# A decoder trunk on one core: the mLSTM stage issued in another order

## The chip, the cores and the metric

The kernel runs on one core of a Trainium2 chip. Its time is the device time of one execution in microseconds (us). Three runs of the kernel before gave 1001.4, 1002.04 and 1003.79 us; their median, 1002.04 us, is what the change is measured against. A difference under 0.3% of it, 3.0 us, is about what a measurement of this kernel can't tell from no change.

Engines are named as the profile names them: PE multiplies matrices (PEld loads its stationary operand), ACT evaluates functions and copies with a scale, DVE is the vector engine, POOL the general-purpose one, SP issues the transfers from memory.

## The reference, cut to what matters

Two layers, 256 tokens of width 1024. Each layer is a feed-forward half step, a token mixer beside a cross-attention, and a second feed-forward half step, every one followed by a layer norm. Layer 1, where the change is, has the mLSTM mixer:

```python
u = x @ w_in_mlstm[j]                       # q, k, v, output gate, 8 gates, cross-attention q
qk = silu(causal_dwconv(qk, qk_conv_w))     # 4 taps
gates = gates + b_gates
log_i, log_f = gates[..., :4], log_sigmoid(gates[..., 4:])
# per head: weights exp(log_d - m_t), log_d = bcum_t - bcum_s + log_i_s for s <= t
sc = einsum('bhtd,bhsd->bhts', q, k) * w_intra
num = einsum('bhts,bhse->bhte', sc, v) + ...
h = num / max(abs(den), exp(-m_t))
h = head_norm(h)
tok = sigmoid(o_pre) * h
mix = concat([tok, cross_attention(q, mem @ w_kv_mem)]) @ w_out
x = layer_norm(alpha * x + mix)
```

## The kernel before, in words

All matrices are fp32. A large product is made of operands split into two exact parts, w_h and w_l (line 98: ACT copies raw to w_h with rounding, line 99; DVE subtracts, line 100), and runs on PE as two or three fp32r products (lines 171 to 182). Small products (attention scores, transposes, decay broadcasts, mLSTM scores and numerators) run as plain fp32, without a split; such a matmul is two PE instructions in the trace.

Weights stream through three raw buffers and five pairs of split buffers, in the order of the list `pieces`; `get` makes the pieces one or two ahead of use. In the mLSTM stage one raw buffer holds the four decay matrices (line 571, `decays`), and another the norm gains (`hnb`) until POOL has multiplied the output gates by them (line 564).

The order on each engine is not written out by hand: the code is recorded in the order in which it is called, and a scheduler of the Tile layer then fixes one sequence for each engine. An engine works through its sequence strictly in order, so an instruction that waits holds all behind it. PSUM has two pools of four banks: `ybank` for long sums and scores, `mbank` for the rest. A bank is given out again when its last reader is done; the reader of a product bank is the pair of `comb` (lines 186 and 187), an ACT copy and a DVE addition.

The mLSTM stage (from line 540; its calls stand in lines 719 to 748) does this:

- output gates and the eight gate columns, then `Xattn`'s query projection (tile xq);
- `gate_rows` (574): a chain of small operations over ACT, DVE and POOL, which leaves running sums and maxima in `rows`;
- `values(h, t)` (697): v, for half h of the heads and token tile t, 24 matmuls of 384 columns (tile v);
- `scores(c)` and `values(c)` of the cross-attention (429, 455): eight instructions of scores each (tile sc), a softmax over ACT and DVE, then transposes (pT) and products (xo);
- `columns` (603): four tiny transposes (tile cols), copied out, and an exponential on ACT;
- `decay(h0)` (612): two heads in one bank; a broadcast matmul with four rows of contraction (tile negm), then for each head two DVE additions of the mask (619), two exponentials (620) and a third (622);
- `qk_piece(n)` (627), six of them, three of k and three of q: two banks of eight product pairs (tile qkp), `comb`, the first tap on ACT (637), three taps on DVE (639), and one silu over both banks on ACT (643);
- `mscores(h)` (648), `numer(t)` (661): scores (tile ms) weighted by the decays, numerators (tile num), denominators and head norm on DVE;
- `tokens(t)` (708): gate times normed head, transposed (tile tk), split into the operand `mix`;
- `OutProj`: `head` (493) multiplies the two chunks of `mix` that come from the cross-attention, `rest` (498) the others (tile yo), with the layer norm half by half.

Of the kernel before, what the change touches and what calls it, by code (L numbers as in the profile page):

```python
# [14 lines left out]
P = 128  # L15
# [16 lines left out]
def trunk(ctx: ExitStack, tc: tile.TileContext, d, out):  # L32
# [23 lines left out]

# [1 line left out]
    pieces = []  # L58

    def downs_after(g, xs):  # L60
        """The groups whose down product follows group g's gate and up."""
        if g < max(xs, 1) or g > NG - TAIL:
            return []
        return list(range(g)) if g == xs else [g - 1]
# [37 lines left out]
    def new_act(name):  # L102
        """[128, chunk, part, token]: the two parts side by side."""
        return actp.tile([P, KC, 2, T], F32R, tag="a", name=name)
# [36 lines left out]

# [1 line left out]
    warm = consts.tile([P, 256], F32R, name="warm")  # L143
# [27 lines left out]
    def mm3(o, a, b, start, stop):  # L171
        """o += a^T b with a, b in two exact parts."""
        ah, al = a
        bh, bl = b
        pe.matmul(o, ah, bh, start=start, stop=False)  # L175
        pe.matmul(o, ah, bl, start=False, stop=False)  # L176
        pe.matmul(o, al, bh, start=False, stop=stop)  # L177

    def mmw(bank, w, a, start, stop):
        """bank = [w_h^T a_h + w_l^T a_h | w_h^T a_l], a's parts side by side."""  # L180
        pe.matmul(bank, w[0], a.rearrange("p c t -> p (c t)"), start=start, stop=False)  # L181
        pe.matmul(bank[:, :T], w[1], a[:, 0], start=False, stop=stop)  # L182

    def comb(o, bank):
        """The sum of a bank's two halves."""
        act.activation(o, bank[:, T:], AF.Copy)  # L186
        dve.tensor_add(o, o, bank[:, :T])  # L187

    def tsl(t):
        return slice(t * P, (t + 1) * P)  # L190
# [3 lines left out]

# [1 line left out]
    def load_ln(i):  # L196
# [46 lines left out]
    def norm_both(i, gb, nx, tail):  # L243
        """tail(t): the last products of tile t; its norm follows, t = 1's transposes later."""
        tr = None
        for t in range(2):
            tail(t)
            tr = ln_finish(i, t, gb, nx)
            if t == 0 and nx is not None:
                tr()  # L250
        cur["x"], cur["pending"] = nx, tr
# [4 lines left out]
    def to_parts(a, k0, n, t, bank):  # L256
        """n chunks of 128 columns, transposed in a bank, into an operand's two parts."""
        bv = bank[:, :n * P].rearrange("p (c t) -> p c t", c=n)
# [3 lines left out]

# [1 line left out]
    def ffn(l, j, xs_groups, i, last=False):  # L264
# [113 lines left out]

# [1 line left out]
    kvs = {}  # L380
# [23 lines left out]
    def proj_ws(w, name, use):  # L404
        """Two 128-column chunks of x @ w, transposed; use(chunk, bank) after each."""
        for c in range(2):
# [66 lines left out]

# [1 line left out]
    ORDER = [6, 7, 0, 1, 2, 3, 4, 5]  # L475

    class OutProj:
# [14 lines left out]

        def head(self):
            self.ws[0] = get("wo", self.l, 0)
            for t in range(2):
                self.part(0, t, (0, 1))

        def rest(self, gb):
            for q in range(1, 4):
# [3 lines left out]
            def tail(t):  # L503
                self.part(1, t, (0, 1))
                for h in range(2):
                    for q in range(2, 4):
# [3 lines left out]

# [1 line left out]
    def conv_mixer(mix, between):  # L512
# [22 lines left out]

# [1 line left out]
    lo, hi, al = slice(0, 64), slice(64, 128), slice(0, 128)  # L537
    HP = [((0, al), (1, lo)), ((1, hi), (2, al)), ((3, al), (4, lo)), ((4, hi), (5, al))]

    def mlstm_mixer(mix, i):  # L540
        hnb = rawp.tile([P, 2048], F32, tag="raw", name="hnb")
        nc.sync.dma_start(hnb[:, :DTOK], bass.AP(tensor=d["hng"].tensor, offset=d["hng"].offset,
                                                 ap=[[0, P], [1, DTOK]]))
        # the output gate, natural; the input and forget gates ride along
        w = [get("wop", q) for q in range(4)]
# [19 lines left out]

        # gates as rows [head, t]
        rows = [zp.tile([P, D], F32, tag="z", name=f"rows{q}").rearrange("p (n t) -> p n t", n=4)
# [6 lines left out]
        def gate_rows():  # L574
# [4 lines left out]
            act.activation(rows[0][:NH, 0:2, :], b[:NH].rearrange("p (m t) -> p m t", m=2), AF.Copy)  # L579
            # log_sigmoid(f) = min(f, 0) - log1p(exp(-|f|)); ln(u) is corrected for u's rounding  # L580
            pool.memset(aa, 1.0)
# [10 lines left out]
            pool.tensor_sub(lf, tt, lf)  # L592
            # running sums and maxima
            dve.tensor_tensor_scan(f, aa, lf, 0.0, op0=ALU.mult, op1=ALU.add)
# [15 lines left out]

        # decay weights, transposed: E[s, t] = exp(a_s - M_t) for t >= s
        def decay(h0):
            nb = mbank(f"negm{h0}")
            for h in (h0, h0 + 1):
                o = nb[:, (h - h0) * T:(h - h0) * T + T]
                pe.matmul(o, ident[:NH, h:h + 1].to_broadcast([NH, P]), e, start=True, stop=True)
                Et = E[h]
                for t in range(2):
                    dve.tensor_add(Et[:, 256 * t:256 * t + P], o[:, tsl(t)], mask)
                    act.activation(Et[:, 256 * t:256 * t + P], Et[:, 256 * t:256 * t + P], AF.Exp,  # L620
                                   bias=cols[:, t, h:h + 1])
                act.activation(Et[:, P:256], o[:, P:], AF.Exp, bias=cols[:, 0, h:h + 1])

        # q and k, convolved, silu'd, transposed: [channel, q or k, chunk, t]
        qk = [hp.tile([P, 2, 2, T], F32, tag="h", name=f"qk{n}") for n in range(3)]
# [31 lines left out]

        # h = num / max(|den|, exp(-m)), head norm
        hn = {}
# [30 lines left out]

        # v, natural, with a column of ones after each head
        v1 = [hp.tile([P, NH, DH + 1], F32, tag="h", name=f"v1_{t}") for t in range(2)]
# [29 lines left out]
        xa.scores(0)  # L722
        values(0, 1)
        xa.scores(1)
        columns()
        decay(0)
        decay(2)
        qk_piece(0)
        xa.values(0)
        qk_piece(1)  # L730
        xa.values(1)
        qk_piece(2)
        qk_piece(3)
        qk_piece(4)
        qk_piece(5)
        values(1, 0)
        mscores(0)
        mscores(1)
        values(1, 1)
        mscores(2)  # L740
        mscores(3)
        numer(0)
        numer(1)
        o = OutProj(1, mix, i)
        tokens(0)
        o.head()
        tokens(1)
        o.rest(load_ln(i))

# [1 line left out]
    def late_loads():  # L751
# [21 lines left out]
    o = OutProj(0, mix, 1)  # L773
    o.head()
    o.rest(gb)
# [5 lines left out]

# [1 line left out]
def _layouts(i):  # L783
# [5 lines left out]
    def colmajor(w, width):  # L789
        """[1024, n*width] -> [n, 128, 8*width]: piece, k in chunk, chunk x column."""  # L790
        n = w.shape[1] // width
# [43 lines left out]
```

## Time and profile before

| What | us |
|---|---|
| median of three runs (1001.4 to 1003.79) | 1002.04 |
| profiled execution, span from first to last instruction | 1004.1 |
| PE busy in it | 986.8 (98%) |
| DVE busy | 664.8 (66%) |
| ACT busy | 530.1 (53%) |

The page gives the span of the profiled execution and no other time of it; it is 2.1 us over the median of the runs and 0.3 us over the longest of them. The mLSTM stage, from the output gates to the first products of the next feed-forward, lies between 680 and 810 us of the span. A busy PE is not PE at its peak: the ends of matmuls are modelled, and the clock granted to PE is a row of its own.

### The profile page before, as it was taken

How to read it: one execution, taken by the hardware profiler on the slowest of the kernel's cores; microseconds unless marked ns; L12 is line 12 of the kernel's file. 1: busy time of each engine (PE TensorE's matmuls, PEld its weight loads, DVE VectorE, ACT ScalarE, POOL GpSimd, SP SyncE). 2: the span in 40 equal slices, each digit the busy share in tenths (PEclk: the TensorE clock that was granted, in tenths of full speed). 3: DMA queues.
4: the chain of work that ended last, by engine and by line, in shares of the span. 5: the costliest groups of instructions: out<-in, count | busy, mean ns of one | idle time of the engine just before them, and what ended most of it. 6: DMA issues, size and time to landing. Idle time of an engine off the chain costs nothing.

```text
span 1004.1 us, 12980 instructions
## 1 busy us (share of the span) xinstructions
PE 986.8 (98%) x5116; PEld 834.7 (83%) x5116; DVE 664.8 (66%) x1010; ACT 530.1 (53%) x851; POOL 39.4 (4%) x52
## 2 busy tenths in 40 slices
PE   8999999999999999999999999999999999999996
PEld 7888888888888888888788888889788788888885
DVE  6685657868677656565866656576478887556555
ACT  6565555447445545556355555535676346454540
POOL 0000000100000000000100000002300110000001
PEclk9999999999999999999999999999799999999999
DMA  8884546455535654644464646434145466546421
GB/s 277 311 295 166 210 168 212 171 228 205 187 130 187 241 201 159 218 155 180 173 246 168 215 162 213 154 111 154 78 149 205 185 236 230 199 158 216 161 84 43
DMA packets 29293, 186.90 MB, mean 186 GB/s; under 512 B 3632, under 2 KB 4656, under 8 KB 8368
## 3 DMA queue, kind: packets, MB, share of 16 engines
q1 hardware_dynamic: 29232, 186.07, 51.7%
q8 instruction: 40, 0.66, 0.2%
q14 instruction: 21, 0.17, 0.1%
HBM read 185.01 MB, written 1.05 MB: 185 GB/s over the span
## 4 chain that ended last, share of the span: by engine, by line
PE 89%; DVE 4%; POOL 2%; DMA 2%; issue 2%; ACT 0%; SPq 0%; POOLq 0%; DVEq 0%; ACTq 0%
PE gu L181 28%; PE gu L182 14%; PE y L177 8%; PE y L175 8%; PE y L176 8%; PE qkp L181 3%; PE gx L175 2%; PE gx L177 2%; PE gx L176 2%; DVE wl L100 1%; PE qkp L182 1%; PE cx L181 1%; PE cg L181 1%; PE cb L181 1%; PE yo L177 1%
## 5 line engine op out<-in xcount | busy, mean ns | idle before, releaser
L100 DVE TENSOR_TENSOR wl<-raw,wh 128x1024 fp32r<-128x1024 f32 (+1 forms) x342 | 400.6, 1195 | 147.6 <-ACT wh L99 146.8
L181 PE MATMUL gu<-x,wh 128*128 128x512 f32 x1216 | 431.1, 399 | 1.4 <-DVE s L187 1.1
L99 ACT ACTIVATE wh<-raw 128x1024 fp32r<-128x1024 f32 (+1 forms) x342 | 338.3, 1032 | 113.4 <-PE y L177 45.0
L182 PE MATMUL gu<-x,wl 128*128 128x256 f32 x1216 | 340.8, 281 | 0.4 <-DVE wl L100 0.2
L181 PEld LDWEIGHTS gu<-x,wh 128*128 128x128 f32 x1216 | 228.5, 188 | 57.4 <-DVE s L187 1.4
L182 PEld LDWEIGHTS gu<-x,wl 128*128 128x128 f32 x1216 | 230.0, 189 | 2.6 <-DVE wl L100 1.0
L175 PE MATMUL y<-wh,h 128*128 128x512 f32 x352 | 138.1, 392 | 0.0
L177 PE MATMUL y<-wh,h 128*128 128x512 f32 x352 | 137.7, 391 | 0.0
L176 PE MATMUL y<-wl,h 128*128 128x512 f32 x352 | 137.2, 390 | 0.0
L187 DVE TENSOR_TENSOR s<-s,gu 128x256 f32<-128x256 f32 x152 | 63.2, 417 | 107.6 <-ACT s L186 107.6
L186 ACT ACTIVATE s<-gu 128x256 f32<-128x256 f32 x152 | 57.4, 379 | 111.4 <-PE gu L182 110.7
L177 PEld LDWEIGHTS y<-wh,h 128*128 128x128 f32 x352 | 66.1, 188 | 14.5
L175 PEld LDWEIGHTS y<-wh,h 128*128 128x128 f32 x352 | 66.1, 188 | 14.0
L176 PEld LDWEIGHTS y<-wl,h 128*128 128x128 f32 x352 | 66.1, 188 | 13.0
L301 ACT ACTIVATE h<-s 128x256 fp32r<-128x256 f32 x76 | 31.7, 417 | 68.2 <-DVE s L298 68.0
L297 ACT ACTIVATE s<-s 128x256 f32<-128x256 f32 x76 | 31.6, 416 | 37.0 <-DVE s L187 37.0
L302 DVE TENSOR_TENSOR h<-s,h 128x256 fp32r<-128x256 f32 x76 | 32.0, 421 | 17.9 <-ACT h L301 17.9
L181 PE MATMUL qkp<-x,wh 128*128 128x512 f32 x96 | 38.6, 438 | 0.0
L175 PE MATMUL gx<-wh,x 128*128 128x512 f32 x96 | 38.2, 398 | 0.2 <-DVE x L261 0.2
L177 PE MATMUL gx<-wh,x 128*128 128x512 f32 x96 | 37.5, 391 | 0.0
L176 PE MATMUL gx<-wl,x 128*128 128x512 f32 x96 | 37.4, 390 | 0.0
L260 ACT ACTIVATE x<-xt 128x512 fp32r<-128x512 f32 x20 | 11.4, 596 | 44.2 <-PE xt L239 43.8
(191 smaller groups left out, 996.1 us busy)
## 6 DMA issues: line engine op xcount, KB each, us to landing
raw<-in_wgu SPq DMA_DIRECT2D x83, 1024.0 KB, 4.8
raw<-in_wd SPq DMA_DIRECT2D x43, 1024.0 KB, 4.8
raw<-in_wconv SPq DMA_DIRECT2D x10, 1024.0 KB, 4.8
raw<-in_wout SPq DMA_DIRECT2D x8, 1024.0 KB, 4.8
raw<-in_wm SPq DMA_DIRECT2D x7, 1024.0 KB, 4.7
gb<-in_lngb SPq DMA_DIRECT2D x6, 1024.0 KB, 4.9
raw<-in_wkv SPq DMA_DIRECT2D x4, 1024.0 KB, 4.9
raw<-in_wop SPq DMA_DIRECT2D x4, 776.0 KB, 4.2
```

Of the source, the lines that this page charges most:

```text
L99: act.activation(h, raw, AF.Copy)
L100: dve.tensor_sub(l, raw, h.bitcast(F32))
L175: pe.matmul(o, ah, bh, start=start, stop=False)
L176: pe.matmul(o, ah, bl, start=False, stop=False)
L177: pe.matmul(o, al, bh, start=False, stop=stop)
L181: pe.matmul(bank, w[0], a.rearrange("p c t -> p (c t)"), start=start, stop=False)
L182: pe.matmul(bank[:, :T], w[1], a[:, 0], start=False, stop=stop)
L186: act.activation(o, bank[:, T:], AF.Copy)
L187: dve.tensor_add(o, o, bank[:, :T])
L297: act.activation(t_[:, :256], t_[:, :256], AF.Silu)
L301: act.activation(hh, t_[:, 256:], AF.Copy)
L302: dve.tensor_sub(hT[g][:, 1, fc, :], t_[:, 256:], hh.bitcast(F32))
```

## The change

The order of the calls of the mLSTM stage is another one. `scores(1)` follows the first q/k piece, `columns` and the four decays are spread between the q/k pieces, one head at a time, and so are `values(0)` and `values(1)` of the cross-attention. The four `mscores` and `numer(0)` follow each other, with `values(1, 1)` between `numer(0)` and `numer(1)`. `head` takes a token tile: that of tile 0 stands ahead of `tokens(0)`, that of tile 1 ahead of `rest`, and `tokens(1)` is called within `rest`, after the second quarter of tile 0. Comments are gone, so lines differ by up to two. The number of matmuls is the same.

```diff
-        def head(self):
-            self.ws[0] = get("wo", self.l, 0)
-            for t in range(2):
-                self.part(0, t, (0, 1))
+        def head(self, t):
+            if t == 0:
+                self.ws[0] = get("wo", self.l, 0)
+            self.part(0, t, (0, 1))
 
-        def rest(self, gb):
+        def rest(self, gb, between=None):
...
             def tail(t):
                 self.part(1, t, (0, 1))
+                if t == 0 and between:
+                    between()
...
-        def decay(h0):
-            nb = mbank(f"negm{h0}")
-            for h in (h0, h0 + 1):
-                o = nb[:, (h - h0) * T:(h - h0) * T + T]
-                pe.matmul(o, ident[:NH, h:h + 1].to_broadcast([NH, P]), e, start=True, stop=True)
-                Et = E[h]
-                for t in range(2):
-                    dve.tensor_add(Et[:, 256 * t:256 * t + P], o[:, tsl(t)], mask)
-                    act.activation(Et[:, 256 * t:256 * t + P], Et[:, 256 * t:256 * t + P], AF.Exp,
-                                   bias=cols[:, t, h:h + 1])
-                act.activation(Et[:, P:256], o[:, P:], AF.Exp, bias=cols[:, 0, h:h + 1])
+        def decay(h):
+            o = mbank(f"negm{h}")[:, :T]
+            pe.matmul(o, ident[:NH, h:h + 1].to_broadcast([NH, P]), e, start=True, stop=True)
+            Et = E[h]
+            for t in range(2):
+                dve.tensor_add(Et[:, 256 * t:256 * t + P], o[:, tsl(t)], mask)
+                act.activation(Et[:, 256 * t:256 * t + P], Et[:, 256 * t:256 * t + P], AF.Exp,
+                               bias=cols[:, t, h:h + 1])
+            act.activation(Et[:, P:256], o[:, P:], AF.Exp, bias=cols[:, 0, h:h + 1])
...
         values(0, 1)
+        qk_piece(0)
         xa.scores(1)
+        qk_piece(1)
         columns()
         decay(0)
+        qk_piece(2)
+        decay(1)
+        xa.values(0)
+        qk_piece(3)
         decay(2)
-        qk_piece(0)
-        xa.values(0)
-        qk_piece(1)
         xa.values(1)
-        qk_piece(2)
-        qk_piece(3)
         qk_piece(4)
+        decay(3)
         qk_piece(5)
         values(1, 0)
-        mscores(0)
-        mscores(1)
+        for h in range(NH):
+            mscores(h)
+        numer(0)
         values(1, 1)
-        mscores(2)
-        mscores(3)
-        numer(0)
         numer(1)
         o = OutProj(1, mix, i)
+        o.head(0)
         tokens(0)
-        o.head()
-        tokens(1)
-        o.rest(load_ln(i))
+        o.head(1)
+        o.rest(load_ln(i), lambda: tokens(1))
```

On PE, where the second scores, the columns and the decay broadcasts stood, just ahead of the first q/k piece, before:

```order
L434 MATMUL sc_10_6040<-kT_1760,xqT_5884 128x256
L434 MATMUL sc_11_6041<-kT_1760,xqT_5884 128x256
L606 MATMUL cols<-ident,rows_5865 128x4
L607 MATMUL cols<-ident,rows_5865 128x4
L606 MATMUL cols<-ident,rows_5865 128x4
L607 MATMUL cols<-ident,rows_5865 128x4
L616 MATMUL negm_6073<-rows_5864,ident 128x256
L616 MATMUL negm_6086<-rows_5864,ident 128x256
L181 MATMUL qkp_0_6109<-x_5562,wh_5955 128x512
```

And with the change, on PE, from the last product of the third q/k piece (wl_6127) to the first products of the fourth (wh_6197), where the second head's broadcast negm_6251 and the transposes of the first attention half now stand:

```order
L182 MATMUL qkp_1_6227<-x_5562,wl_6127 128x256
L616 MATMUL negm_6251<-rows_5864,ident 128x256
L463 MATMUL pT_00_6259<-ident,p_00_5996 128x128 x4
L463 MATMUL pT_01_6267<-ident,p_01_6006 128x128 x4
L181 MATMUL qkp_0_6287<-x_5562,wh_6197 128x512
L468 MATMUL xo_0_6258<-p_00_5996,vm_1761 64x256 x2
L182 MATMUL qkp_0_6287<-x_5562,wl_6198 128x256
```

The scores, columns and broadcasts that stood in one block are now apart, each behind a q/k piece; the scheduler gives pT_00 the bank of the first head's broadcast, and pT_01 the bank of the second head's, negm_6251, so that each waits until DVE and ACT have read that broadcast.

On ACT, the exponentials of the decays (lines 620 and 622) before, with the first copy of a q/k piece (line 186) and its first tap (637) among them:

```order
L609 ACTIVATE ecol<-cols 128x8
L620 ACTIVATE decays<-decays,cols 128x128 x2
L622 ACTIVATE decays<-negm_6073,cols 128x128
L620 ACTIVATE decays<-decays,cols 128x128 x2
L622 ACTIVATE decays<-negm_6086,cols 128x128
L186 ACTIVATE qu_6100<-qkp_0_6109 128x256
L620 ACTIVATE decays<-decays,cols 128x128 x2
L622 ACTIVATE decays<-negm_6073,cols 128x128
L637 ACTIVATE qr_6099<-qu_6100,qcw 128x256
L620 ACTIVATE decays<-decays,cols 128x128 x2
L622 ACTIVATE decays<-negm_6086,cols 128x128
```

With the change, on ACT, from the end of the second q/k piece to the last exponential of the second head (L643 is the silu of a piece, wh_6197 the split of the fourth piece's weights):

```order
L611 ACT_TABLE_LOAD
L611 ACTIVATE ecol<-cols 128x8
L620 ACTIVATE decays<-decays,cols 128x128 x2
L643 ACT_TABLE_LOAD
L643 ACTIVATE qk_5870<-qr_6123 128x512
L622 ACT_TABLE_LOAD
L622 ACTIVATE decays<-negm_6187,cols 128x128
L99 ACTIVATE wh_6197<-raw_6196 128x1024 x2
L186 ACTIVATE qu_6195<-qkp_0_6204 128x256
L186 ACTIVATE qu_6195<-qkp_1_6227 128x256
L620 ACTIVATE decays<-decays,cols 128x128 x2
L622 ACTIVATE decays<-negm_6251,cols 128x128
```

The exponentials, which stood together ahead of the first silu, now alternate with the silus, and the function tables are loaded at each turn: in the mLSTM stage ACT's sequence holds 12 table loads after the output gates where it held 4.

On PE, around the first transposes of the gated heads (tk), before:

```order
L176 MATMUL yo_11_6687<-wl_6489,mix_5705 128x512
L715 MATMUL tk_6648<-ident,og 128x128 x3
L177 MATMUL yo_11_6687<-wh_6488,mix_5705 128x512
L175 MATMUL yo_00_6669<-wh_6662,mix_5705 128x512
L715 MATMUL tk_6655<-ident,og 128x128 x3
L176 MATMUL yo_00_6669<-wl_6663,mix_5705 128x512
```

With the change, at the same place on PE:

```order
L175 MATMUL yo_01_6661<-wh_6490,mix_5705 128x512
L176 MATMUL yo_01_6661<-wl_6491,mix_5705 128x512
L177 MATMUL yo_01_6661<-wh_6490,mix_5705 128x512
L715 MATMUL tk_6672<-ident,og 128x128 x3
L715 MATMUL tk_6679<-ident,og 128x128 x3
L175 MATMUL yo_10_6685<-wh_6490,mix_5705 128x512
```

Before, 23 products of the out-projection stood ahead of the first tk, all of them `head`; now 12 do, those of tile 0, and 40 stand between the transposes of tile 0 and those of tile 1, where 26 stood.

## Rows read from the trace of the kernel before

**Rows 1.** The page: busy time by engine, and the granted clock over 40 slices of the span (in tenths of full speed).

```profile
PE 986.8 (98%) x5116; PEld 834.7 (83%) x5116; DVE 664.8 (66%) x1010; ACT 530.1 (53%) x851; POOL 39.4 (4%) x52
...
PEclk9999999999999999999999999999799999999999
```

**Rows 2.** The view by windows, PE alone: stretch, its length, PE busy (instructions), granted clock, share of the transfer engines, GB/s.

```profile
713.82:717.34 3.52, 2.74 (x16) 1.00 0.00 0
717.34:730.99 13.65, 13.65 (x38) 0.50 0.00 0
730.99:767.58 36.59, 36.59 (x220) 1.00 0.49 163
775.31:782.67 7.36, 7.36 (x41) 1.00 0.48 156
```

**Rows 3.** The timeline of PE: start, duration, line, tiles, count, and the idle time ahead with what ended it.

```profile
713.82 0.70 PE L434 MATMUL sc<-kT,xqT 64*128 64x256 f32 x2
714.97 1.13 PE L434 MATMUL sc<-kT,xqT 64*128 64x256 f32 x6 [0.45 <-ACT p L446]
716.58 0.22 PE L607 MATMUL cols<-ident,rows 4*128 4x4 f32 x1 [0.34 <-POOL rows L598]
716.79 1.52 PE L616 MATMUL negm<-rows,ident 4*128 4x256 f32 x4
719.69 0.63 PE L181 MATMUL qkp<-x,wh 128*128 128x512 f32 x1
720.33 0.63 PE L181 MATMUL qkp<-x,wh 128*128 128x512 f32 x1
...
723.02 1.22 PE L616 MATMUL negm<-rows,ident 4*128 4x256 f32 x2
...
725.11 1.22 PE L616 MATMUL negm<-rows,ident 4*128 4x256 f32 x2
...
735.94 0.40 PE L181 MATMUL qkp<-x,wh 128*128 128x512 f32 x1
736.30 0.40 PE L181 MATMUL qkp<-x,wh 128*128 128x512 f32 x1
```

**Rows 4.** Groups of ACT's instructions in the stretch 713.82 to 767.58: line, operation, tiles, shapes, count, then busy time, mean ns of one, idle time ahead and its releaser.

```profile
L99 ACT ACTIVATE wh<-raw 128x1024 fp32r<-128x1024 f32 (+1 forms) x16 | 15.6, 1001 | 0.6 <-DMA raw<-in_wm 0.6
L637 ACT ACTIVATE qr<-qu,qcw 128x256 f32<-128x256 f32 x12 | 6.1, 505 | 0.7 <-DVE qu L187 0.6
L186 ACT ACTIVATE qu<-qkp 128x256 f32<-128x256 f32 x12 | 4.6, 380 | 10.1 <-PE qkp L182 10.1
L643 ACT ACTIVATE qk<-qr 128x512 f32<-128x512 f32 x5 | 3.1, 628 | 0.1
L620 ACT ACTIVATE decays<-decays,cols 128x128 f32<-128x128 f32 x8 | 2.8, 398 | 0.0
L465 ACT ACTIVATE p<-pT 128x512 f32<-128x512 f32 x4 | 2.2, 591 | 0.1
L622 ACT ACTIVATE decays<-negm,cols 128x128 f32<-128x128 f32 x4 | 1.4, 360 | 0.0
L643 ACT ACT_TABLE_LOAD x1 | 1.3, 1283 | 1.1 <-DVE qr L639 1.1
```

**Rows 5.** The timeline of ACT in the gate chain: a table load and the activation behind it.

```profile
704.92 1.28 ACT L583 ACT_TABLE_LOAD   x1
706.22 0.42 ACT L583 ACTIVATE rows<-rows 4x256 f32<-4x256 f32 x1
```

**Rows 6.** The timeline of DVE: the operations of the softmax, of a q/k piece and of the gate chain.

```profile
714.11 0.68 DVE L596 TENSOR_TENSOR_SCAN rows<-rows 4x256 f32<-4x256 f32 x1 [0.25 <-POOL rows L595]
...
715.48 1.20 DVE L451 TENSOR_SCALAR p<-p,ri 128x256 f32<-128x256 f32 x2
...
717.32 1.28 DVE L441 TENSOR_REDUCE nm<-sc 128x2 f32<-128x512 f32 x2
...
725.63 0.42 DVE L187 TENSOR_TENSOR qu<-qu,qkp 128x256 f32<-128x256 f32 x1 [0.86 <-ACT qu L186]
...
726.86 1.52 DVE L639 SCALAR_TENSOR_TENSOR qr<-qu,qcw,qr 128x253 f32<-128x253 f32 x3
```

**Rows 7.** The timeline of PE where the mLSTM scores, the values between them and the numerators stand.

```profile
767.58 3.73 PE L654 MATMUL ms<-qk 128*128 128x256 f32 x16
771.07 0.42 PE L175 MATMUL v<-wh,x 128*128 128x384 f32 x1
...
775.31 3.73 PE L654 MATMUL ms<-qk 128*128 128x256 f32 x16
778.88 4.09 PE L673 MATMUL num<-v,decays 128*128 128x193 f32 x24
782.67 0.53 PE L175 MATMUL yo<-wh,mix 128*128 128x512 f32 x1
```

**Rows 8.** The timeline of PE around the transposes of the gated heads, and the first product of the feed-forward behind.

```profile
789.13 0.52 PE L715 MATMUL tk<-ident,og 128*128 128x128 f32 x3 [0.89 <-DVE og L712]
...
790.23 0.50 PE L175 MATMUL yo<-wh,mix 128*128 128x512 f32 x1 [0.35 <-DVE og L712]
...
797.72 0.99 PE L715 MATMUL tk<-ident,og 128*128 128x128 f32 x6 [0.73 <-DVE og L712]
...
809.71 0.40 PE L175 MATMUL gx<-wh,x 128*128 128x512 f32 x1
```

More of the change, by code (lines that the diff above doesn't have):

```diff
@@ L773, in trunk @@
     o = OutProj(0, mix, 1)
-    o.head()
+    o.head(0)
+    o.head(1)
     o.rest(gb)
```

## The prediction

> **What bounds the kernel now.** I read the page first: PE is busy for 98% of the span, and the row of its granted clock shows one slice of 40 at seven tenths [rows 1]. So nothing but PE sets the end, and a change of order can win only where PE stood, or ran at the lower of its two levels, 1.2 in place of 2.4 GHz. The windows find that stretch: from 717.34 to 730.99 the granted clock was 0.50, 13.65 us long, with PE busy throughout [rows 2]. The timeline shows what came just before: the second scores, an idle 0.45 us for ACT, the tiny column transposes, 0.34 us for POOL, and the broadcasts with four rows of contraction; PE was busy for 2.74 of 3.52 us [rows 2, 3]. The third view is the end of the stage, where PE waits for the gated heads on DVE, 0.89, 0.35 and 0.73 us [rows 8].
>
> **What the new order takes away.** A product pair took 0.64 us at the low level (719.69 to 720.33) and 0.36 at the high one (735.94 to 736.30) [rows 3]. Of the 38 instructions in the slow stretch 31 are qkp, 15.5 pairs or 5.5 us at the high level. The other 7 are broadcasts: 0.36 us apart at the stretch's start (1.45 us for four, to 718.24, partly slow already); the mLSTM scores, 128 and 256 columns mixed, stood 0.22 apart (3.49 us for 16) [rows 3, 7]. I take 0.30, so 2.1 us. The stretch cost 13.65 - 7.6 = 6.1 us. With both idle times, 6.9 us are to be had.
>
> **What it adds.** Exponentials and silus alternate, so that ACT loads tables 12 times in place of 4; behind the second v product it is 9 in place of 1. One load took 1.283 us [rows 4], so 10.3 us more of ACT in all. ACT has the room in sum: it waited for PE in this stretch for 10.1 us [rows 4]. But it works in order, and PE's banks hang on it, so I walked the new sequences of PE, ACT and DVE side by side with the durations of rows 3, 4 and 6 (times as if on the old span; PE reaches the end of the second v product at 713.8 as before).
>
> PE: first piece to 719.5, scores to 720.7, second piece to 726.4, columns and broadcast to 727.6, third piece to 733.3, second broadcast to 734.1. The third piece needs a bank that DVE frees at 727.0: no wait, by 0.6 us.
>
> DVE (durations from [rows 6]): the splits of the second and third piece's weights now stand ahead of the gate chain, which starts its first exponential at 709.1 in place of 706.2 [rows 5], and the first softmax sums come at 714.4. From there DVE does four multiplications of 0.6, two scans of 0.65, two additions of 0.4, six taps of 0.4, two reductions of 0.6 and three waits for ACT or POOL (0.65, 0.5, 0.5), with smaller ones, and ends the first piece's taps at 724.1.
>
> ACT from 724.1: table 1.28, silu 0.63, copy 0.35, wait for DVE's second softmax until 727.0, tap 0.5, copy 0.35, wait until 728.35, tap 0.5, table 1.28, exponentials behind their masks until 731.0, table 1.28, silu 0.6, table 1.28, the first head's last exponential at 734.65. Then two splits of 1.0, two copies of 0.36, two exponentials of 0.3, and the second head's last one at 738.3.
>
> PE again: pT_00 waits for the 734.65, 0.6 us; pT_01 for the 738.3, 3.15 us; the second pair of xo waits for its copy, which stands behind a split and two taps on ACT (741.25), 0.65 us; the fifth piece waits 0.5 us for a bank of the fourth. Together 4.9 us. The values (4.24 us [rows 7]) then end at 765.3, where before they ended at 767.58.
>
> The clock comes in again here. From 733.4 to 738.9 PE has a four-row broadcast, transposes and 3.75 us of idle time, more than ahead of the fall at 717.34 [rows 2]. I therefore take a second fall. Its price lies between nothing and a repeat of the whole 6.1 us. I take the piece that follows, 5.64 us of products at half speed for about three fifths of it: 3.3 us, less 0.8 of the waits named, which a slower PE no longer feels: 2.5. The values then end at 767.8, 0.2 later than before.
>
> There is a cap on the best case. The last silu, which the third mLSTM scores need, comes at 768.2 in my walk of ACT. Before, without the values between, they would have started at 775.31 - 4.24 = 771.1 [rows 7]. While ACT's chain stays so, the stage can't win more than 2.9 us.
>
> Scores, values and numerators took 15.09 us (767.58 to 782.67 [rows 7]). Four scores in a row and half the numerators are 7.15 + 1.4 us of plain fp32; scores and numerators in a row, 7.36 us, held the granted clock at 1.00 [rows 2]. Same parts, so nothing.
>
> The end of the stage wins: numer(0) starts 4.24 us before numer(1), so DVE has the first gated head some 2.8 us behind the last numerator, about when the 12 products of tile 0 (2.75 us: 26 of them and three transposes filled 790.23 to 796.99 [rows 8], and I take 0.23 each) are done; I leave 0.3 us. The second tile has 40 products, 9.1 us, ahead of its transposes in place of 26; I find DVE done at 794.1 on the old clock, just before them. Of 1.97 us [rows 8] 0.3 stays; another 0.3 goes where fewer products cover the transposes of the normed tile ahead of 809.71. That is -1.4 us. Bounds: nothing, and the whole 1.97.
>
> The first layer's PE sequence is unchanged, and the weights' transfers keep their order; two are issued earlier, which costs nothing while the engines' share in the slow stretch was 0.00 [rows 2].
>
> Sum: +0.2 - 1.4 = -1.2 us. On the profiled span that is 1002.9 of 1004.1; the span stands 2.1 us over the median, so on the median it is 1002.04 - 1.2 = 1000.8.
>
> **A rule that speaks against it.** In this trace the activation behind a load starts 1.30 us after the load starts (704.92 to 706.22) [rows 5], so a switch costs its row. The Trainium skill, page "ScalarE: Activation LUTs", section "What ACT_TABLE_LOAD costs", adds a drain of about 1.38 us to each load of 1.283. The trace agrees with the load and shows no drain. By the page, eight more switches would be an estimated 21 us of ACT in place of 10.3.
>
> **The rivals.**
>
> *The clock holds* (0.22). PE stays at 1.00 through the wait for pT_01. For it: at 788 to 797 idle times of 0.35 to 0.89 left the clock alone. Against: these waits are longer. Then the values end at 765.3: -2.3 - 1.4 = -3.7, 998.3.
>
> *ACT hides its tables* (0.10). If ACT reaches the second head's last exponential by 735, because what I put in series overlaps, PE sees neither wait nor fall, and all comes: -6.9 - 1.4 = -8.3, 993.7. For it: ACT's 10.1 us of waiting in the old order. Against: the chain from 724.1 to 738.3 holds 1.5 us of waits, the rest is work.
>
> *The fall lasts* (0.17). Before, the clock stayed low while single broadcasts cut the products (723.02 and 725.11 [rows 3]), and came back only behind an uncut row of them. In the new order the fourth piece is cut by two pairs of xo, and a broadcast and transposes follow. If the low level reaches past the end of the fourth piece (746), the whole 6.1 is paid again, 3.6 more than I took: +2.4, 1004.4, slower than before.
>
> *A switch costs more than its row* (0.04). The one load ahead of a silu came behind 1.05 us of idle time on ACT, named as a wait for DVE [rows 4]. If ACT must stand for that long at each switch, nine make 9.5 us, the last silu comes at 777.7, 6.6 behind the 771.1, and the end is +6.6 - 1.4 = +5.2, 1007.2. The page named above is this rival's source; the 1.30 us of rows 5 is why it gets so little.
>
> **How the numbers follow.** The forecast, stalls on ACT and a short fall, has 0.47, with 998.5 to 1003 as its own range. A difference of 3.0 us (0.3%) is what the measurement can tell. Faster by more: two thirds of the first rival, the second, and a twentieth of the forecast, 0.15 + 0.10 + 0.05 = 0.30. Slower by more: under half of the third and the fourth, with 0.01 for the forecast, 0.08 + 0.04 + 0.01 = 0.13. The rest, 0.57, is no change that can be told. The range for 8 in 10 leaves out the second rival, the fourth and the outer part of the third: 996.0 to 1005.0.
>
> **What would show it.** Right: nine table loads on ACT between the second v product and the last silu; PE idle before pT_01 by about 3 us with ACT's line 622 as releaser; a granted clock of 0.50 right behind it, shorter than 13.65 us, and none near the first q/k piece; under 0.7 us of idle time left before the tk. Wrong: no wait at pT_01 (then the walk of ACT is wrong), or a clock of 1.00 through it (then the first rival), or a low stretch as long as before.

## The result, and the profile after

The changed kernel took 1005.62 us (median of seven runs, 1004.57 to 1007.44), the kernel before 1001.40 beside it (seven runs, 999.48 to 1003.79): a ratio of 1.0041, with a 95% interval of 1.0027 to 1.0056. It is slower by some 4.2 us; forecast were 1000.8 us in a range of 996.0 to 1005.0, and slower by over 0.3% had a chance of 0.13.

The profiled execution of the changed kernel took 1004.82 us, 1.9 of them outside its span of 1002.9. Of the seven it has the highest mean granted clock, 0.996; the others show 0.993 to 0.995, so the usual execution of the changed kernel runs longer at half clock than the trace read here. Its page, the lines that answer to [rows 1]:

```profile
PE 983.2 (98%) x5116; PEld 830.4 (83%) x5116; DVE 667.3 (67%) x1010; ACT 540.8 (54%) x859; POOL 38.2 (4%) x52
...
PEclk9999999999999999999999999999999999999999
```

ACT has 8 instructions more, the table loads, and 10.7 us more to do. The slice at seven tenths is gone, and the kernel is slower all the same. The windows of PE (length, PE busy, granted clock, share of the transfer engines, GB/s) show a shorter fall in another place than in [rows 2]:

```profile
720.00:731.15 11.15, 10.40 (x60) 1.00 0.00 1
731.15:735.90 4.75, 1.35 (x7) 1.00 0.00 0
735.90:739.30 3.40, 3.06 (x9) 0.50 0.55 188
739.30:766.13 26.83, 26.55 (x145) 1.00 0.36 128
```

From 731.15 on PE is busy for 1.35 of 4.75 us, and behind that runs at half clock for 3.40 us. The timeline of PE says what it stands for (start, duration, line, tiles, count, and the idle time ahead with what ended it); it answers to [rows 3]:

```profile
701.11 0.60 PE L580 MATMUL grows<-ident,gn 128*4 128x128 f32 x4
...
723.88 0.67 PE L616 MATMUL negm<-rows,ident 4*128 4x256 f32 x2
...
725.30 0.50 PE L181 MATMUL qkp<-x,wh 128*128 128x512 f32 x1 [0.75 <-DVE qu L187]
...
731.15 0.69 PE L616 MATMUL negm<-rows,ident 4*128 4x256 f32 x2
...
732.97 0.66 PE L463 MATMUL pT<-ident,p 128*128 128x128 f32 x4 [1.12 <-ACT decays L622]
...
736.24 1.12 PE L463 MATMUL pT<-ident,p 128*128 128x128 f32 x4 [2.62 <-ACT decays L622]
...
737.72 1.83 PE L468 MATMUL xo<-p,vm 128*64 128x256 f32 x4
...
740.84 1.08 PE L468 MATMUL xo<-p,vm 128*64 128x256 f32 x4
```

Both transposes of the first attention half (pT) wait for the decays' last exponentials on line 622. The timeline of ACT shows why these are late (table loads have no tiles); the pair of [rows 5] now stands here at every turn:

```profile
722.60 1.28 ACT L643 ACT_TABLE_LOAD   x1
723.89 0.63 ACT L643 ACTIVATE qk<-qr 128x512 f32<-128x512 f32 x1
...
729.31 1.28 ACT L643 ACT_TABLE_LOAD   x1
730.60 0.63 ACT L643 ACTIVATE qk<-qr 128x512 f32<-128x512 f32 x1
731.25 1.28 ACT L622 ACT_TABLE_LOAD   x1
732.55 0.37 ACT L622 ACTIVATE decays<-negm,cols 128x128 f32<-128x128 f32 x1
732.82 1.99 ACT L99 ACTIVATE wh<-raw 128x1024 fp32r<-128x1024 f32 x2
...
735.82 0.37 ACT L622 ACTIVATE decays<-negm,cols 128x128 f32<-128x128 f32 x1
```

At 729.31 ACT changes to the silus' table for one silu of 0.63 us and at 731.25 back to that of the exponentials; a split of weights (L99) follows. The groups of ACT between 711 and 766 us, the counterpart of [rows 4], have nine loads where one stood:

```profile
L643 ACT ACT_TABLE_LOAD x5 | 6.4, 1283 | 0.1
...
L620 ACT ACT_TABLE_LOAD x2 | 2.6, 1283 | 0.0
...
L611 ACT ACT_TABLE_LOAD x1 | 1.3, 1283 | 0.0
L622 ACT ACT_TABLE_LOAD x1 | 1.3, 1283 | 0.0
```

At the end of the stage PE still waits for the gated heads, 0.73 and 1.19 us, 1.92 in all, against 1.97 in [rows 8]:

```profile
785.02 1.12 PE L715 MATMUL tk<-ident,og 128*128 128x128 f32 x6 [0.73 <-DVE dn L676]
...
796.44 0.99 PE L715 MATMUL tk<-ident,og 128*128 128x128 f32 x6 [1.19 <-DVE og L712]
```

The timeline of DVE has the reason for the 1.19: a split of weights (L100) stands between the norm of the second tile's heads (L687) and their gate (L712). Ahead of the first tile's gate no split stands there; DVE waited 1.26 us for POOL's root, as it did for the second tile.

```profile
782.89 1.25 DVE L687 TENSOR_SCALAR ht<-ht,hmv,hn0r 128x192 f32<-128x192 f32 x4 [1.26 <-POOL hn0r L206]
...
793.44 1.25 DVE L687 TENSOR_SCALAR ht<-ht,hmv,hn1r 128x192 f32<-128x192 f32 x4 [1.26 <-POOL hn1r L206]
794.60 1.22 DVE L100 TENSOR_TENSOR wl<-raw,wh 128x1024 fp32r<-128x1024 f32 x1
795.74 1.02 DVE L712 TENSOR_TENSOR og<-og,ht 128x384 f32<-128x384 f32 x2
```

### The profile page after: what moved, and what is told of

Its sections match the earlier page's. It is cut to its first block, busy times and chain, and to the rows that moved or that the text cites. A ratio compares the mean times of both kernels' runs of the same rounds, so it can differ in the third digit from the quotient of the medians.

```text
span 1002.9 us, 12987 instructions
## 1 busy us (share of the span) xinstructions
PE 983.2 (98%) x5116; PEld 830.4 (83%) x5116; DVE 667.3 (67%) x1010; ACT 540.8 (54%) x859; POOL 38.2 (4%) x52
## 3 DMA queue, kind: packets, MB, share of 16 engines
HBM read 185.01 MB, written 1.05 MB: 186 GB/s over the span
## 4 chain that ended last, share of the span: by engine, by line
PE 88%; DVE 4%; ACT 3%; DMA 2%; POOL 2%; issue 1%; POOLq 0%; DVEq 0%; ACTq 0%
PE gu L181 28%; PE gu L182 14%; PE y L177 8%; PE y L175 8%; PE y L176 8%; PE gx L177 2%; PE gx L176 2%; PE gx L175 2%; PE qkp L181 1%; PE cx L181 1%; PE cb L181 1%; PE cg L181 1%; DMA raw<-in_wm 1%; PE xt L239 1%; PE kb L181 1%
## 5 line engine op out<-in xcount | busy, mean ns | idle before, releaser
L100 DVE TENSOR_TENSOR wl<-raw,wh 128x1024 fp32r<-128x1024 f32 (+1 forms) x342 | 400.6, 1195 | 149.5 <-ACT wh L99 148.8
L99 ACT ACTIVATE wh<-raw 128x1024 fp32r<-128x1024 f32 (+1 forms) x342 | 338.3, 1032 | 112.9 <-PE y L177 48.4
L181 PE MATMUL qkp<-x,wh 128*128 128x512 f32 x96 | 35.0, 405 | 1.0 <-DVE qu L187 1.0
```

Of the source, the lines that this page charges most:

```text
L99: act.activation(h, raw, AF.Copy)
L100: dve.tensor_sub(l, raw, h.bitcast(F32))
```

## The experiments

All are read between three points of PE's timeline: the transposes of the gates (grows), the first of the mLSTM scores (ms), and the first product of the feed-forward behind the stage (gx). "Waits" is the idle time of PE that the timeline names between the first and the last point; "clock" is half the length of the stretches at the granted clock of 0.50. Times in us of each run's profiled execution.

| kernel | grows to ms | ms to gx | sum | waits | clock | ratio to before, 95% |
|---|---|---|---|---|---|---|
| before, the prediction's trace | 63.90 | 42.13 | 106.03 | 2.8 | 6.8 | |
| e1, before again | 59.81 | 42.13 | 101.94 | 3.2 | 1.7 | 0.9993 [0.9982, 1.0004] |
| after | 65.02 | 42.49 | 107.51 | 6.9 | 1.7 | 1.0041 [1.0027, 1.0056] |
| e2, old end | 65.45 | 43.70 | 109.15 | 6.4 | 3.4 | 1.0066 [1.0052, 1.0079] |
| e3, one table | 59.11 | 42.47 | 101.58 | 3.2 | 0 | 0.9982 [0.9971, 0.9994] |
| e4, silus last | 58.56 | 41.64 | 100.20 | 2.5 | 0 | 0.9984 [0.9973, 0.9995] |
| e5, only the end | 59.83 | 41.83 | 101.66 | 2.8 | 1.7 | 0.9991 [0.9979, 1.0003] |
| e6, pT elsewhere | | | 105.91 | 5.2 | 0 | 1.0048 [1.0029, 1.0066] |
| e7, e4 and the gate | 57.77 | 40.87 | 98.64 | 1.0 | 0 | 0.9952 [0.9936, 0.9968] |
| e8, e4 with the old end | 58.28 | 43.80 | 102.08 | 4.4 | 0 | 0.9998 [0.9985, 1.0011] |

(In e6 the first scores stand among the values, so its sum isn't parted.) By the 0.3% that a measurement can tell, e1, e3, e4, e5 and e8 can't be told from the kernel before; the changed kernel, e2 and e6 are slower, e7 is faster. Against the changed kernel's ratio e3 and e4 are 0.6% faster.

### e1: the kernel before, once more

No edit.

> The kernel before, unchanged, run again. The prediction took all it could win from one profiled execution: a stretch of 13.65 us at half clock (6.1 us lost) and, behind 10 us, a start that looks late beside the changed kernel's (first gate rows at 703.68 against 701.11 us). Theory A, that execution was no typical one: this profile starts its gate rows at about 701, its own time lies within 1.5 us of 1001.4, and its slow stretch is shorter than 13 us or absent; the mean clock of the timed runs is above 0.991 in most. Rival B, it was typical: gate rows at 703.7 again, a slow stretch of 13 to 14 us, mean clock 0.991 in nearly all runs, and the own time near 1006.

The profiled execution took 999.6 us, and its gates came at 701.40. PE's windows around the second scores and broadcasts, and the rows of its timeline that answer to [rows 3] and [rows 7]:

```profile
714.86:720.60 5.74, 5.34 (x25) 1.00 0.00 0
720.60:724.20 3.60, 3.60 (x13) 0.53 0.00 0
724.20:761.21 37.01, 37.01 (x222) 1.00 0.48 161
```

```profile
712.69 1.13 PE L434 MATMUL sc<-kT,xqT 64*128 64x256 f32 x6 [0.45 <-ACT p L446]
...
718.68 0.69 PE L616 MATMUL negm<-rows,ident 4*128 4x256 f32 x2 [0.40 <-ACT decays L622]
...
726.59 1.19 PE L468 MATMUL xo<-p,vm 128*64 128x256 f32 x8
...
761.21 2.90 PE L654 MATMUL ms<-qk 128*128 128x256 f32 x12
```

The same program, the same order, the same 0.45 us of waiting: but the clock falls within the 3.60 us of the second window, whose mean of 0.53 makes 3.4 us at 0.50, and not for 13.65 us [rows 2]; that costs 1.7 us. The results list the mean granted clock of every timed execution too. Of 63 of the kernel before, taken with e1 to e4 and with e5 to e8, 43 had 0.995 or more and a median of 999.97 us; 20 had 0.994 or less and a median of 1002.8; three had 0.991, the value of the prediction's trace, and took 1003.88 to 1005.41. The 0.996 of the trace above is the commonest value, in 35 of the 63. So theory A holds, but for the own time, which is 1.8 us from 1001.4 where it had 1.5 at most: if 0.991 stands for the long fall, that is one execution in about twenty. The first trace's span of 1004.1 stands for about 1006 us, if what lies around the span is 1.8 to 2.2 us as in every one of these. That is above each of the three runs it was set beside.

### e2: the changed kernel with the old end

```diff
-        for h in range(NH):
-            mscores(h)
-        numer(0)
-        values(1, 1)
-        numer(1)
+        mscores(0)
+        mscores(1)
+        values(1, 1)
+        mscores(2)
+        mscores(3)
+        numer(0)
+        numer(1)
         o = OutProj(1, mix, i)
-        o.head(0)
         tokens(0)
+        o.head(0)
         o.head(1)
-        o.rest(load_ln(i), lambda: tokens(1))
+        tokens(1)
+        o.rest(load_ln(i))
```

> The changed kernel with the end of the stage as before (scores in pairs around the last values, both numerators together, the gated heads ahead of head). Theory A (the loss is in front, on ACT's queue): the end is worth nothing either way, idle time ahead of the tk 1.9 us as in both traces; time within 1 us of the changed kernel's 1005.6. Rival C (the new end is what costs): 1002.5 or less. The prediction's own term (the new end wins 1.4 us): 1007.

1006.9 us, ratio 1.0066. Rival C is out: the new end is not what costs. Theory A's time, within 1 us of 1005.6, is missed by 0.3. From ms to gx the old end took 43.70 us here and the new one 42.49, 1.2 us for the new end, near the prediction's 1.4. But the ratios' intervals, 1.0052 to 1.0079 and 1.0027 to 1.0056, overlap a little, so that the times alone don't part this from nothing. Two things come on top. The front had a second stretch at half clock, between 726.0 and 729.4, behind a wait of 1.02 us ahead of the third piece where the changed kernel had 0.75 and no fall, as the windows of PE show:

```profile
726.00:729.40 3.40, 3.40 (x12) 0.50 0.02 5
```

And the old end took 1.6 us more here than in the kernel before (42.13, in both of its traces).

### e3: one table for exponentials and silus

```diff
-            act.activation(qk[i][:, which].rearrange("p c t -> p (c t)"), r, AF.Silu)
+            act.activation(qk[i][:, which].rearrange("p c t -> p (c t)"), r, AF.Exp)
```

> The changed kernel with an exponential where the six silus of q and k stand (this changes what is computed: q and k are exp of the convolution in place of silu), so that exponentials and 'silus' share one table. Order of PE as in the changed kernel. Theory A: no table loads between the second v product and the last of the six; pT_00 and pT_01 wait under 0.8 us together (3.74 in the changed kernel), no half clock around 736 us, so about 3.0 + 1.7 us less: 1000.5 to 1001.5. Rival D (the tables are not what holds ACT): waits over 2.5 us stay, 1004 or more.

999.03 us, ratio 0.9982. With PE's order as in the changed kernel, but for a few places (the eight products xo of an attention half now stand together), and no table load between the second v product and the last of the six, both waits ahead of pT are gone, and so is the fall. The windows of PE, and the transposes and products of the first attention half in its timeline:

```profile
730.00:740.00 10.00, 8.91 (x51) 1.00 0.35 115
```

```profile
731.21 1.09 PE L463 MATMUL pT<-ident,p 128*128 128x128 f32 x8
...
733.38 1.57 PE L468 MATMUL xo<-p,vm 128*64 128x256 f32 x8 [1.08 <-ACT p L465]
```

From grows to ms it takes 59.11 us, 5.9 less than the changed kernel. Rival D is out: this shows that the turns between the tables are the cause, and that without them the new order of PE is no slower than the old one. It is not free: without the wait of 1.08 us, the attention's transposes and products take 5.1 us in this trace from start to start and 3.7 in e1; that there is no fall (1.7 us in e1), and 0.7 us less for the scores, makes up for it. The time came out 1.5 us below what I expected: the kernel before took 1000.18 us beside it, 1.2 less than beside the changed kernel, and the eight products of xo take 1.57 us here, where four of them took 1.83 in the changed kernel.

### e4: the true silus, behind the decays

```diff
-            r = tmp(f"qr{n}")
+            r = qk[i][:, which].rearrange("p c t -> p (c t)")
...
-            act.activation(qk[i][:, which].rearrange("p c t -> p (c t)"), r, AF.Silu)
+        zb = sp.tile([P, 1], F32, tag="zb", name="zb", bufs=1)
+
+        def silu(n):
+            if n == 0:
+                dve.tensor_scalar(zb, E[3][:, P:P + 1], 0.0, None, op0=ALU.mult)
+            r = qk[n % 3][:, 1 if n < 3 else 0].rearrange("p c t -> p (c t)")
+            act.activation(r, r, AF.Silu, bias=zb)
...
         decay(0)
+        decay(1)
         qk_piece(2)
-        decay(1)
+        decay(2)
         xa.values(0)
         qk_piece(3)
-        decay(2)
+        decay(3)
         xa.values(1)
+        for n in range(4):
+            silu(n)
         qk_piece(4)
-        decay(3)
+        silu(4)
         qk_piece(5)
+        silu(5)
```

The zero bias hangs on the last head's decay, so that the scheduler, which takes what is ready, can't put a silu among the exponentials.

> The changed kernel with the true silus, but held behind the last decay (a zero column made from the last head's decay is their bias; the convolution is written into the q/k tile itself and the silu done in place) and with the decays one q/k piece earlier (0 and 1 behind the second piece, 2 behind the third, 3 behind the fourth): one table load for silu in place of nine loads. Theory A: PE waits under 1.5 us in all between the second v product and the scores, no half clock; 999.5 to 1001.5. Rival E (small fp32 matmuls at four places let the clock fall whatever ACT does): a half-clock stretch of 3 us or more appears, 1003 or more.

998.79 us, ratio 0.9984: 0.7 us below the range of theory A, and 0.16% below the kernel before, less than a measurement can tell. All that PE waits for, in its timeline:

```profile
726.56 0.50 PE L181 MATMUL qkp<-x,wh 128*128 128x512 f32 x1 [0.82 <-DVE cols L610]
...
734.28 1.56 PE L468 MATMUL xo<-p,vm 128*64 128x256 f32 x8 [0.25 <-ACT p L465]
...
779.46 0.55 PE L722 MATMUL tk<-ident,og 128*128 128x128 f32 x3 [0.50 <-DVE og L719]
...
789.83 0.99 PE L722 MATMUL tk<-ident,og 128*128 128x128 f32 x6 [0.96 <-DVE og L719]
```

No half clock in this trace, though small fp32 matmuls stand at four places: rival E is out for it. What theory A says of the waits (1.07 us between the second v product and the scores) and of the clock holds, with the computation unchanged.

### e5: the kernel before with the new end

The end of e2's diff the other way round, and `head` and `rest` as in the change.

> The kernel before with only the end of the stage changed (four scores and numer(0) ahead of the last values, head per token tile, the second tile's heads within rest). The first queue of the stage is as before, so ACT has one table load there. The prediction gave the new end -1.4 us, bounds 0 and -1.97: ratio 0.9986. Theory F (the new end is worth nothing, since DVE puts splits of weights ahead of the gated heads): ratio 0.9993 to 1.0007, 1.5 to 2.2 us of idle time ahead of the tk. Rival C (the new end costs): above 1.001.

Ratio 0.9991, 0.9979 to 1.0003: the interval holds the prediction's 0.9986 and theory F's nothing, and leaves out rival C. From ms to gx 0.3 us less than before (41.83 against 42.13), with 1.65 us ahead of the tk in place of 1.97. Inconclusive between the two.

### e6: the transposed attention weights in other banks

```diff
-                tb = mbank("pT" + n)
+                tb = ybank("pT" + n)
```

> The changed kernel with the transposed attention weights (pT) in banks of the other PSUM pool, so that they wait for no decay's last exponential; the table loads stay, 8 or 9 of them. Theory G (the loads cost PE only through the bank that pT shares with a broadcast): the 3.74 us ahead of pT go, no half clock near 736, 1000 to 1001.5. Rival H (ACT's queue is the bound, and whatever comes behind it on ACT makes PE wait: the copies of pT, of the q/k pieces, the last silus): PE waits 3 us or more elsewhere, 1003.5 or more.

1006.26 us, ratio 1.0048: as slow as the changed kernel. The timeline of PE, and what ACT does then:

```profile
732.51 0.66 PE L463 MATMUL pT<-ident,p 128*128 128x128 f32 x4
...
734.65 0.49 PE L181 MATMUL qkp<-x,wh 128*128 128x512 f32 x1 [1.48 <-ACT wh L99]
...
735.91 0.39 PE L182 MATMUL qkp<-x,wl 128*128 128x256 f32 x1 [0.76 <-DVE wl L100]
```

```profile
732.00 1.28 ACT L622 ACT_TABLE_LOAD   x1
733.29 0.37 ACT L622 ACTIVATE decays<-negm,cols 128x128 f32<-128x128 f32 x1
733.56 1.99 ACT L99 ACTIVATE wh<-raw 128x1024 fp32r<-128x1024 f32 x2
```

pT no longer waits for line 622, but PE goes on to the next piece, whose weights ACT splits behind the same table loads, and waits there for 2.24 of the 3.74 us. In the trace, which has no half clock, 1.6 us are won between grows and gx (105.91 against 107.51); the runs show nothing of it. Theory G falls by its time; rival H is the nearer one, with 2.9 us of waits ahead of the last score and 5.2 in all. The bank was where the wait showed, and ACT's queue what most of it was for.

### e7: e4, the columns in another bank, and the gate ahead of the root

```diff
-            cb = mbank("cols")
+            cb = ybank("cols")
...
-                dve.tensor_scalar(ht[:, s], ht[:, s], mv[:, h, 0:1], rs[:, h:h + 1],
-                                  op0=ALU.subtract, op1=ALU.mult)
-            hn[t] = ht
+                dve.scalar_tensor_tensor(ht[:, s], ht[:, s], mv[:, h, 0:1], ogs[t][:, s],
+                                         op0=ALU.subtract, op1=ALU.mult)
+            hn[t] = ht, rs
...
-                dve.tensor_mul(og[:, s], og[:, s], hn[t][:, s])
+                ht, rs = hn[t]
+                dve.tensor_tensor(og[:, s].rearrange("p (a e) -> p a e", a=2),
+                                  ht[:, s].rearrange("p (a e) -> p a e", a=2),
+                                  rs[:, 2 * h:2 * h + 2, None].to_broadcast([P, 2, DH]), op=ALU.mult)
```

> The version with the silus behind the decays, and two more edits: the column transposes stand in a bank of the other pool, so that the third piece no longer waits for their copy (0.82 us), and the gate multiplies the centred heads while POOL still computes the square roots, so that behind POOL's wait only one multiplication by the root is left (about 1.1 us in place of 2.27). Theory F (the end hangs on DVE behind POOL): idle time ahead of the tk from 1.46 to under 0.6 us, 1.0 to 1.8 us below the version without the two edits, so about 997.3. Rival I (DVE is busy with splits of weights anyway, and only their order changes): within 0.5 us of 998.8.

996.56 us, ratio 0.9952 with 0.9936 to 0.9968: faster than both kernels, by 4.5 us against the runs of before beside it (1001.09). PE's waits for the gated heads in its timeline, and DVE ahead of the second:

```profile
777.57 0.94 PE L725 MATMUL tk<-ident,og 128*128 128x128 f32 x6
...
787.06 0.99 PE L725 MATMUL tk<-ident,og 128*128 128x128 f32 x6 [0.79 <-DVE og L720]
```

```profile
786.35 1.03 DVE L720 TENSOR_TENSOR og<-ht,hn1r 128x384 f32<-128x384 f32 x2 [0.94 <-POOL hn1r L206]
```

Of the 1.46 us 0.79 are left, not under 0.6, and the 0.82 ahead of the third piece are gone; between grows and gx it is 1.56 us shorter than e4. By the times it is 2.2 us below e4, more than the 1.0 to 1.8 expected; five of e4's executions show a mean clock of 0.996 and none of e7's is under 0.997, so part of that may be the clock. Theory F is the nearer one.

### e8: e4 with the old end

The end as in e2's diff.

> The version with the silus behind the decays, and the end of the stage as before. It prices the end where the front makes PE wait for nothing. Theory F (the end is worth nothing): within 0.7 us of 998.8. The prediction's term: 1000.2, 1.4 us above. Rival C (the new end costs): 998 or less.

1001.22 us, ratio 0.9998 against e4's 0.9984: 1.4 us for the new end, as the prediction's term has it, though the intervals overlap. The timeline of PE has longer waits of the kind of [rows 8]:

```profile
782.22 0.52 PE L722 MATMUL tk<-ident,og 128*128 128x128 f32 x3 [1.12 <-DVE og L719]
...
783.80 0.52 PE L722 MATMUL tk<-ident,og 128*128 128x128 f32 x3 [1.06 <-DVE og L719]
...
788.93 0.50 PE L177 MATMUL yo<-wh,mix 128*128 128x512 f32 x1 [0.72 <-DVE mix L261]
```

Rival C is out here too. The old end takes 43.80 us behind this front and 43.70 behind that of e2, but 42.13 behind the old one. Most of it is PE waiting longer for DVE: the named waits behind the first score are 3.4 us here and 2.8 in e2, against 2.0 before. What makes DVE late there is open; no run here takes it apart.

## Why the prediction was wrong

**The step that failed** is the first term of the sum: "The stretch cost 13.65 - 7.6 = 6.1 us. With both idle times, 6.9 us are to be had." It is right for the execution it was read from, and not for the kernel. The other trace of before loses 1.7 us to its fall, and e1's list of executions, with its mean clock of 0.996 in 35 of 63, says that this is the usual one. So 4.4 us of the 6.1 were not there to be won. From grows to ms the kernel before needs 59.81 us and not 63.90; against the prediction's 64.1 for the changed kernel (63.90 + 0.2) that alone is +4.3 where it had +0.2. With the -1.4 for the end left as it was, the sum is +2.9 us: 1004.3 on the 1001.40 of the runs beside the changed kernel, close to the 1005.62 measured.

The last step hid this: "the span stands 2.1 us over the median, so on the median it is 1002.04 - 1.2". A span and a time were set against each other as if they were the same quantity. With what lies around the span the profiled execution was some 4 us over its median, which should have been explained, not subtracted. Against e1 it is 4.1 us longer between grows and gx, in the very term I was about to spend, and its gates came 2.3 us later; 1.9 of these had gathered in the first 24 us of the span, where PE's named waits are 1.6 us in this trace and 0.45 in e1's, far from the change.

**What held.** The walk of ACT's queue: nine table loads; the last exponential of the first head at 732.92 and that of the second at 736.19 on the new clock, 732.1 and 735.7 by the prediction (its 734.65 and 738.3, less the 2.57 us by which the gates came earlier). Waits of 1.12 and 2.62 us at pT, 3.74 together, where it had 0.6 and 3.15, 3.75 together. A second fall shorter than the first, 3.40 us long, so 1.7 lost in this trace where 2.5 was taken as a net cost; the median of the seven mean clocks, 0.995, stands for some 1 us more. Scores, values and numerators: 15.11 us from the first score to the first product of the out-projection (766.13 to 781.24), 15.09 before [rows 7].

**What else was off.** The third piece was to wait for nothing, with 0.6 us to spare; it waited 0.75 for a bank whose copy on ACT came behind a table load and a silu (722.60 to 724.5), since the softmax kept ACT until 722.6, 1.1 us later than in my walk. The fifth piece waited 0.28, where I had 0.5, and the second pair of xo waited for nothing, where I had 0.65. So it is partly luck that the waits of the front add up to 4.77 us, near the 4.9 of the prediction. Together the changed kernel's front is 65.02 us, 0.9 above the prediction.

**The end** was to win 1.4 us and came out 0.36 longer than before (42.49 against 42.13). Where only the end differs, the traces give the new end 1.2 us (e2 and after), 2.2 (e8 and e4) and 0.3 (before and e5): a gain each time, but of no one size. What I left out is that it does not add to the front's: behind the new front the old end would have been 1.6 us longer. In the trace the idle time did not fall from 1.97 to 0.3 but stayed at 1.92. Of that 1.19 comes from the split of weights that DVE's order has in front of the second tile's gate. The first tile's 0.73 has no split behind it: the first gated head was done at 784.87, 3.6 us behind the last numerator (the out-projection starts at 781.24) and not 2.8, and in that time DVE stood 1.26 us for POOL's root.

**The balance.** Against e1 the changed kernel is 5.57 us longer from grows to gx (5.2 by the two executions' own times). The end is 0.36 of that. In the front the named waits are 3.6 us more (4.77 against 1.18); the attention's transposes and products take 6.6 us from start to start and not 3.7, 2.9 more, since the half clock now lies on them and the products xo, parted into two groups, take longer even at full clock (four of them 1.08 us at 740.84, all eight 1.19 in e1); the q/k products, on which the half clock lay before, take 0.7 less, the scores 0.7 less, the broadcasts and columns 0.2 more. That is 3.6 + 2.9 - 0.7 - 0.7 + 0.2 = 5.3, and the front is 5.2 longer.

**The rivals.** "The clock holds" and "ACT hides its tables" did not come: the clock fell, and pT waited. "The fall lasts" had nearly the right time, 1004.4, by a mechanism that did not happen: the fall was over at 739.3, 2.3 us into the fourth piece (from 737.01), not past its end. "A switch costs more than its row" is refuted: ahead of the five loads for a silu ACT stood 0.1 us in all, where the rival had 1.05 at each switch, and behind each load the next activation starts 1.29 or 1.30 us after it (722.60 to 723.89, 731.25 to 732.55). The drain that the Trainium skill, page "ScalarE: Activation LUTs", section "What ACT_TABLE_LOAD costs", adds to a load is not in these rows either. Nine loads at their row's price, in a queue that PE's banks and weights hang on, were enough.

**Two sums of the prediction** do not fit, and neither decides: 6.9 us to be had less 4.9 of waits is 2.0, where the walk has 2.3 (765.3 against 767.58); and a twentieth of 0.47 is 0.02, not the 0.05 that went into the 0.30 for "faster".

## What to carry to other kernels

Before a loss read from one profiled execution is spent as a gain, set that execution's own time, span and what lies around it, against the median of the runs, and explain what is over: a clock fall that varies between executions is worth its usual length, not the length in the page. When matmuls are spread apart on PE, follow what the spreading does to the engine behind them: exponentials and silus that take turns made ACT load tables nine times in place of once, and without the turns nearly the same order of PE (e3, e4) was 0.6% faster than the changed kernel and no slower than the one before. A wait named at a bank goes away with the bank only if the engine that frees it has nothing else that PE needs; in e6 2.24 of its 3.74 us came back at the next two products.

## What the runs showed that I had not expected

The clock's fall belongs to the execution as much as to the program. The kernel before, with the same instructions, fell for 13.65 us in one trace, 0.8 us behind its waits of 0.45 and 0.34 us; in the other it went past the same two (0.45 and 0.33) and fell for 3.4 us later on, 2.1 us behind a third of 0.40. And 20 of its 63 listed executions show a mean granted clock of 0.994 or less. e4 has no fall in its trace, yet of its 11 executions five show 0.996 and six 0.998. What decides between them no run here shows.

A wait of 0.75 us behind columns and one broadcast left the clock at 1.00 in the changed kernel, and one of 1.02 us at the same place in e2 was followed, 0.9 us later, by 3.4 us at half clock; in e6 waits of 1.48 and 0.76 us left it at 1.00. Three traces are too few for a rule.
